# Sparse attention's blocks in another order, the memory branch's output weights kept on chip, and the attention branch's output projection cut into four parts, three of them between the attention blocks

## The chip, the cores and the metric

The kernel runs on one core of one Trainium2 chip. The metric is the device time of one execution in microseconds (us); lower is better.

## The reference, cut to what matters

One layer of an encoder step for 1024 prompt tokens and 64 sample tokens, all in float32. A projection feeds three branches and three gates:

```python
qa, ka, va, qi, ki, wi, ub, qm, gates = project_inputs(x, ...)
a = dsa_attend(qa, qi, wi, pos, ka, va, ki, topk)   # sparse attention: 8 heads of 64, 2 kv heads,
                                                    # keys = top 256 by an index score, chunk-causal
b = pool_mix(ub, ...)                               # trailing means over 2/4/8/16 frames
m = memory_attend(qm, mk, mv)                       # 4 heads of 128 over 256 memory tokens
ga, gb, gm = split(sigmoid(gates))
mixed = ga * (a @ w_oa) + gb * (b @ w_ob) + gm * (m @ w_om)
x = x + mixed @ w_out
h = rmsnorm(x, g_ffn)
y = x + (silu(h @ w_gate) * (h @ w_up)) @ w_down
```

`w_oa` and `w_om` are 512 x 1024, `w_out` 1024 x 1024; the keys, values and index keys are returned as well.

## The kernel before

Every float32 product runs as three products of a rounded high part and a remainder (hi x hi, hi x lo, lo x hi): `matmul3`, L120. A weight block comes by DMA into `raw` (3 buffers), `round_hi` makes `whi` (on POOL in the stage at hand, L96; on POOL or ACT later), and `lo_of` (L86, on DVE) makes `wlo`; `wblock` does all three, with two buffers each for `whi` and `wlo`. All DMAs are issued by SP in the order in which they stand on it. A scheduler places the instructions; each engine then runs its own list in order.

Activations are stored transposed, 128 channels by 1088 tokens, so a matmul streams tokens: 512, 384, 320, 288 or 256 columns. The stages that matter, in order:

1. Projections, index scores, top-k selection, pooling, memory attention, with gate matmuls as filling on TensorE. The memory branch's output sits in `bh`/`bl` (hi and lo).
2. **Memory merge units** (`fill_om(f, ci)`, L571): for one of 8 channel blocks `f` and one of 3 token chunks `OCH` (384, 384, 320 tokens) it loads gate and partial sum (`gt`, 4 buffers) from `side_m`, does 12 matmuls `bh`/`bl` x `w_om` into the bank `fl`, then DVE multiplies (L580), POOL adds (L581), and a DMA stores to `side_a`. There are 24, and the weights of a pair of blocks are loaded again for every chunk (12 loads). One unit runs ahead of the attention, three at its start, one behind each softmax.
3. **Sparse attention**, token blocks of 128 in the order 2, 0, 1, 3, 8, 4, 5, 6, 7 (block 8 is the 64 sample tokens; block b has 128(b+1) keys, block 8 has 192). For each block the queries are split and transposed (`queries_t`: ACT copy, DVE subtraction L879, 8 PE transposes L882, ACT copy). Then for each of the two kv heads a unit of two parts. `softmax`: PE logits L903 for 4 heads, on DVE one instruction that adds the selection and takes the extremum (L907, out `pr`), ACT exp L909, POOL reciprocal L911 and normalisation L913. `values`, which runs one unit behind: for each 128 keys 4 PE transposes (L926) into a bank, ACT copy `ph` L929, DVE remainder `pl` L86, two matmuls into `acc` L933; at its end ACT copies L935/L936, DVE adds L937/L938, ACT copy into `bh` L941 and DVE remainder into `bl`. The attention result overwrites the memory branch's in `bh`/`bl`, so a chunk's memory units must be done before. PSUM has 8 banks: 4 for `tr`, 2 for `mm`, one each for `fl` and `acc`. Once the memory units have run out, every third transposed block of `values` goes to `fl`.
4. **Attention merge** (L996 to L1010), after all blocks: for each `f` one load of gate and sum for all 1088 tokens (`side`, 3 buffers), and for 4 token chunks `ACH` (256, 256, 288, 288) 12 matmuls with `w_oa`, two DVE operations (L1005, L1006), ACT copy L1009 and DVE remainder into `mixed`, split into two token sets: 512 tokens (0) and 576 (1). As soon as the attention's memory is free, SP also issues the residual input (`y`, 16 loads, L990).
5. `out_proj(0)` and `out_proj(1)`: `mixed @ w_out` for a token set; the first needs all 8 channel blocks of `mixed` set 0. Then the norm and the feed-forward part to the end.

## Time and profile before

| | |
|---|---|
| three runs, us | 1764.99, 1768.73, 1771.66; median 1768.73 |
| profiled execution, us | 1774.77; its span 1772.7 |
| granted TensorE clock, mean of the span | 0.993 |
| busy: PE, PE weight load, DVE, ACT, POOL, us | 1719.6, 1668.6, 1124.5, 813.6, 409.5 |

The span is the stretch of one execution that the profiler covers, from the first to the last instruction; some 2 us lie around it. "Busy" of PE counts an instruction from its start to a modelled end, and matmuls overlap in the array, so it is more than the time that the array needs. "Idle before" a group is time in which its engine had nothing running, with what ended it.

### The profile page before, as it was taken

Reading aid. Unit: us, or ns where it says so; the run is one execution under the profiler, and the core shown is the slowest. Engines: PE = TensorE matmul, PEld = TensorE weight load, DVE = VectorE, ACT = ScalarE, POOL = GpSimd, SP = SyncE. Lnnn points to the kernel's source line nnn. Section 1 sums busy time; section 2 is a strip of 40 time slices with the busy share of each in tenths; the row PEclk is TensorE's granted clock in tenths of the full one; section 3 lists DMA queues with packets and bytes.
Section 4 is the critical chain, followed back from the end, with each engine's and each line's share of the span. In section 5 each row is a group of like instructions: output and inputs, shape, how many; then the busy total and the mean of one; then the engine's idle time right before and its main releaser. Section 6 shows DMA issues by size and latency. Waiting matters only on the chain.

```text
span 1772.7 us, 31533 instructions
## 1 busy us (share of the span) xinstructions
PE 1719.6 (97%) x11810; PEld 1668.6 (94%) x11810; DVE 1124.5 (63%) x2411; ACT 813.6 (46%) x1927; POOL 409.5 (23%) x444
## 2 busy tenths in 40 slices
PE   6999999999999998989899999999999999999999
PEld 6999999999999998877798999999999999999999
DVE  6567999999954433778783887544444454544443
ACT  5456677737523432569631354433333333433332
POOL 4111414355412213765203432110000000000000
PEclk9999999999999998999999999999999999999999
DMA  7222441232475336650354333222222221867673
GB/s 231 61 67 73 161 130 46 78 90 98 118 200 190 104 99 207 194 158 1 130 209 137 111 115 130 85 74 74 74 76 89 79 74 43 312 185 244 184 229 98
DMA packets 128582, 224.26 MB, mean 127 GB/s; under 512 B 23463, under 2 KB 86303, under 8 KB 128430
## 3 DMA queue, kind: packets, MB, share of 16 engines
q1 hardware_dynamic: 128430, 222.26, 39.0%
q8 instruction: 93, 1.52, 0.4%
q14 instruction: 59, 0.48, 0.1%
HBM read 167.84 MB, written 54.37 MB: 125 GB/s over the span
## 4 chain that ended last, share of the span: by engine, by line
PE 76%; DVE 11%; ACT 3%; issue 3%; DMA 3%; POOL 2%; SPq 0%; DVEq 0%; ACTq 0%; POOLq 0%
PE mm L1127 24%; PE mm L120 17%; PE mm L1275 15%; PE fl L120 13%; DVE junk_v L780 2%; ACT junk_a L777 2%; PE acc L933 1%; PE tr L903 1%; PE mm L333 1%; DVE wlo L86 1%; PE mm L926 1%; DMA gt<-side_m 1%; DVE lo L86 1%; DVE pl L86 1%; DVE tmlo L86 1%
## 5 line engine op out<-in xcount | busy, mean ns | idle before, releaser
L1127 PE MATMUL mm<-hi,whi 128*128 128x288 f32 (+1 forms) x1120 | 323.2, 289 | 1.1 <-DVE tu L1141 1.1
L1127 PE MATMUL mm<-hi,wlo 128*128 128x288 f32 (+1 forms) x1120 | 324.2, 290 | 0.0
L1127 PE MATMUL mm<-lo,whi 128*128 128x288 f32 (+1 forms) x1120 | 323.5, 289 | 0.0
L1127 PEld LDWEIGHTS mm<-hi,whi 128*128 128x128 f32 x1120 | 211.8, 189 | 1.8 <-DVE tu L1141 1.6
L1127 PEld LDWEIGHTS mm<-lo,whi 128*128 128x128 f32 x1120 | 211.8, 189 | 0.0
L1127 PEld LDWEIGHTS mm<-hi,wlo 128*128 128x128 f32 x1120 | 211.2, 189 | 0.4 <-DVE wlo L86 0.4
L120 PE MATMUL fl<-hh,whi 128*128 128x362 f32 (+1 forms) x576 | 189.7, 330 | 0.9 <-ACT hh L133 0.9
L120 PE MATMUL fl<-hl,whi 128*128 128x362 f32 (+1 forms) x576 | 189.8, 330 | 0.0
L120 PE MATMUL fl<-hh,wlo 128*128 128x362 f32 (+1 forms) x576 | 189.6, 330 | 0.0
L1275 PE MATMUL mm<-uh,wh 128*128 128x362 f32 (+1 forms) x512 | 167.4, 328 | 0.0
L1275 PE MATMUL mm<-ul,wh 128*128 128x362 f32 (+1 forms) x512 | 166.8, 326 | 0.0
L1275 PE MATMUL mm<-uh,wl 128*128 128x362 f32 (+1 forms) x512 | 166.0, 326 | 0.0
L86 DVE TENSOR_TENSOR wl<-raw,wh 128x1024 fp32r<-128x1024 f32 x64 | 78.4, 1225 | 123.4 <-ACT wh L94 123.3
L94 ACT CAST wh<-raw 128x1024 fp32r<-128x1024 f32 x64 | 67.3, 1051 | 145.6 <-PE mm L1275 137.5
L120 PE MATMUL mm<-tmlo,hh 128*128 128x256 f32 (+3 forms) x432 | 122.9, 286 | 1.5 <-DVE tmlo L86 1.5
L120 PE MATMUL mm<-tmhi,hh 128*128 128x256 f32 (+3 forms) x432 | 122.1, 288 | 2.0 <-POOL tmhi L96 2.0
L120 PE MATMUL mm<-tmhi,hl 128*128 128x256 f32 (+3 forms) x432 | 122.6, 286 | 0.0
L86 DVE TENSOR_TENSOR wlo<-raw,whi 128x1024 fp32r<-128x1024 f32 (+1 forms) x75 | 75.9, 1022 | 63.4 <-ACT whi L1119 37.5
L777 ACT ACTIVATE junk_a<-score,cand_a,sgn_a 128x512 f16<-128x512 f32 (+2 forms) x93 | 95.5, 1027 | 42.1 <-DVE cand_a L794 21.8
L120 PEld LDWEIGHTS fl<-hh,whi 128*128 128x128 f32 x576 | 108.3, 188 | 1.7 <-POOL rs L125 1.1
L120 PEld LDWEIGHTS fl<-hl,whi 128*128 128x128 f32 x576 | 108.2, 188 | 0.6
L120 PEld LDWEIGHTS fl<-hh,wlo 128*128 128x128 f32 x576 | 108.2, 188 | 0.5
(386 smaller groups left out, 4545.1 us busy)
## 6 DMA issues: line engine op xcount, KB each, us to landing
raw<-in_w_down_dram SPq DMA_DIRECT2D x66, 512.0 KB, 3.8
fraw<-in_w_gates_dram SPq DMA_DIRECT2D x24, 512.0 KB, 3.7
raw<-in_w_up_dram SPq DMA_DIRECT2D x22, 512.0 KB, 3.8
fr<-in_w_gate_dram SPq DMA_DIRECT2D x18, 512.0 KB, 3.7
side<-side_a SPq DMA_DIRECT2D x8, 1088.0 KB, 6.3
raw<-in_w_out_dram SPq DMA_DIRECT2D x16, 512.0 KB, 3.7
uf<-u SPq DMA_DIRECT2D x44, 181.0 KB, 3.7
u<-tg SPq DMA_DIRECT2D x22, 288.0 KB, 2.1
```

The lines of the kernel that those rows point to most:

```text
L86: V.tensor_tensor(lo, src, hi.bitcast(F32), op=OP.subtract)
L94: A.copy(hi, src)
L120: PE.matmul(ps, l, r, start=i == 0, stop=i == n - 1)
L333: PE.matmul(ps[:n, :cn], qt[:, h, :n], kstack[:, k0 + c:k0 + c + cn], start=True, stop=True)
L777: A.activation(junk[:n, :nk], sc, AF.Sign, bias=bj, scale=1.0 if scale is None else scale[:n, j:j + 1], accum_out=sj)
L780: V.tensor_scalar(junk[:n, :nk], sc, bj, None, op0=OP.is_ge, op1=OP.add, accum_out=sj)
L903: PE.matmul(lg[:n, i * 512:i * 512 + cn], qT[:, h, :n], kT[:, kv, s, k0 + c:k0 + c + cn], start=s == 0, stop=s == 1)
L926: PE.transpose(pt[:cn, i * n:(i + 1) * n], probs[i][:, c:c + cn], ident[:n, :n])
L933: PE.matmul(acc, vv, r, start=ji == 0 and i == 0, stop=ji == nj - 1 and i == 1)
L1127: PE.matmul(dst[i], l, r, start=start and j == 0, stop=stop and j == 11, skip_group_check=True)
L1275: PE.matmul(acc[f], l, r, start=kb == 0 and j == 0, stop=kb == NF - 1 and j == 2)
```

## The change

- The blocks run in the order 8, 6, 7, 2, 0, 1, 5, 4, 3; all keys are loaded ahead of the first or right behind its queries.
- The 24 memory merge units go by chunks 2, 0, 1, one more runs at the start, and two (three for block 2) behind each softmax. The weights `w_om` of a pair of blocks are loaded once and stay for the three chunks: 4 loads instead of 12, half of them in new tiles.
- 24 of the 32 attention merge units (chunks 3, 0 and 2 of `ACH`) move between the attention units, as the table `AFTER` says: `merge_unit` loads gate and sum into `ms` (4 buffers, in the memory weights' tiles), does its 12 matmuls into `fl`, DVE multiplies, POOL adds, and the sum is stored to `mix_d`. Each chunk loads its `w_oa` again: 16 loads instead of 4. While units are left, `values` uses `mm` alone.
- After the attention only chunk 1 (tokens 256 to 511) is merged; the sums of tokens 0 to 255 come back from `mix_d` in the same loop, those of 512 to 1087 inside `out_proj(0)` (`second_mixed`).
- Two remainders (`qs`, `bl`) and the add of the last merge move from DVE to POOL; `pr` has 10 buffers instead of 11; the queries come into `raw`.

```diff
     def fill_om(f, ci, other=False):
-        if f % 2 == 0:
-            om_w[ci] = wblock(a["w_om"][f:f + 2].rearrange("f p k j -> p f k j"), (2, 4, 128))
-        ow = om_w[ci]
+        if f not in om_w:
+            raw = raw_tile()
+            hi, lo = split_tiles() if f < 4 else [kv_p[0].tile([128, 1024], F32R, name=f"om{nm}{f}", tag=f"om{nm}{f}", bufs=1) for nm in "hl"]
...
+            om_w[f] = om_w[f + 1] = [t.rearrange("p (f k j) -> p f k j", f=2, k=4) for t in (hi, lo)]
+        ow = om_w[f]
...
-    rest = [(f, ci) for ci in range(3) for f in range(KT)]
+    OM_ORDER = (2, 0, 1)
+    rest = [(f, ci) for ci in OM_ORDER for f in range(KT)]
...
-    load_keys(0, 384)
+    load_keys(SEQ, SEQ + PAST + DEC)
+    load_keys(0, 512)
...
+    mix_d = dram.tile([KT, 128, T], F32, name="mix_d")
+    mrg = [(f, cc) for cc in (3, 0, 2) for f in range(KT)]
...
-    KEYS_AT = {0: (384, 768), 3: (768, SEQ + PAST + DEC)}
+    KEYS_AT = {8: (512, SEQ)}
...
-            return ap_.tile([128, 1024], F32, name=name, tag="pr", bufs=11)
+            return ap_.tile([128, 1024], F32, name=name, tag="pr", bufs=10)
...
-            q = ap_.tile([128, HA, HDA], F32, name="q", tag="q", bufs=2)
+            q = raw_tile()[:, :512].rearrange("p (h d) -> p h d", h=HA)
...
-            V.tensor_tensor(qs[:n, :, 1], q[:n], qs[:n, :, 0].bitcast(F32), op=OP.subtract)
+            G.tensor_tensor(qs[:n, :, 1], q[:n], qs[:n, :, 0].bitcast(F32), op=OP.subtract)
...
-                    pt = mm() if rest or ji % 3 != 2 else fps(512)
+                    pt = mm() if rest or mrg or ji % 3 != 2 else fps(512)
...
-                lo_of(aol[:, cs, t0:t0 + n], av, aoh[:, cs, t0:t0 + n])
+                G.tensor_tensor(aol[:, cs, t0:t0 + n], av, aoh[:, cs, t0:t0 + n].bitcast(F32), op=OP.subtract)
...
+        MS_TAGS = [f"om{nm}{f}" for f in (4, 6) for nm in "hl"]
+
+        def merge_unit(f, cc):
+            if (f, cc) not in oa_w:
+                oa_w[f, cc] = oa_w[f + 1, cc] = wblock(a["w_oa"][f:f + 2].rearrange("f p k j -> p f k j"), (2, 4, 128))
+            ow = oa_w[f, cc]
+            c0, cn = ACH[cc]
+            tag = MS_TAGS[len(mrg) % 4]
+            t = kvp.tile([128, 1024], F32, name="ms", tag=tag, bufs=1)[:, :2 * cn].rearrange("p (s t) -> p s t", s=2)
+            SP.dma_start(t, side_a[f, :, :, c0:c0 + cn].rearrange("s p t -> p s t"))
+            ps = fps(cn)
+            matmul3(ps, [(ow[0][:, f % 2, k], ow[1][:, f % 2, k], aoh[:, k, c0:c0 + cn], aol[:, k, c0:c0 + cn]) for k in range(4)])
+            V.scalar_tensor_tensor(t[:, 0], t[:, 0], 1.0, ps, op0=OP.add, op1=OP.mult)
+            G.tensor_tensor(t[:, 1], t[:, 1], t[:, 0], op=OP.add)
+            SP.dma_start(mix_d[f, :, c0:c0 + cn], t[:, 1])
...
-        for b in (2,0,1,3,8,4,5,6,7):
+        AFTER = {(0, 0): 2, (0, 1): 2, (1, 0): 2, (1, 1): 2, (5, 0): 1, (5, 1): 1, (4, 0): 2, (4, 1): 2, (3, 0): 4, (3, 1): 6}
+        for b in (8, 6, 7, 2, 0, 1, 5, 4, 3):
             qT = queries_t(b)
...
-                fill(-1, 1)
+                fill(-1, {2: 3}.get(b, 2))
+                merges(AFTER.get(todo[:2], 0))
...
+    c0, c1 = ACH[1][0], ACH[2][0]
     for f in range(KT):
-        sides = row.tile([128, 2, T], F32, name="side", tag="side", bufs=3)
-        SP.dma_start(sides, side_a[f].rearrange("s p t -> p s t"))
+        sides = row.tile([128, 3, 256], F32, name="side", tag="side", bufs=4)
+        SP.dma_start(sides[:, :2], side_a[f, :, :, c0:c1].rearrange("s p t -> p s t"))
+        SP.dma_start(sides[:, 2], mix_d[f, :, :c0])
...
+        keep_mixed(f, 0, c0, sides[:, 2])
+        G.tensor_tensor(pin, pin, gt, op=OP.add)
+        keep_mixed(f, c0, c1, pin)
...
+    def second_mixed(f):
+        pin = y0p.tile([128, 576], F32, name="pin", tag="pin", bufs=3)
+        SP.dma_start(pin, mix_d[f, :, c1:])
+        keep_mixed(f, c1, T, pin)
...
-    sq0 = out_proj(0)
+    sq0 = out_proj(0, {f: lambda f=f: second_mixed(f) for f in range(KT)})
```

What moves, at three places. **POOL**, around the softmaxes of blocks 0 and 1 (lines 911 and 913 before are 921 and 923 now). Before:

```order
L911 TENSOR_TENSOR sm<-sm,mone 128x4
L96 TENSOR_SCALAR whi<-raw 128x1024
L913 TENSOR_SCALAR pr<-pr,sm 128x128 x4
L581 TENSOR_TENSOR gt<-gt 128x384 x2
L911 TENSOR_TENSOR sm<-sm,mone 128x4
L913 TENSOR_SCALAR pr<-pr,sm 128x128 x4
```

The same place now (`ms` is a merge unit's gate and sum, `bl` the attention result's remainder, `qs` the queries'):

```order
L923 TENSOR_SCALAR pr<-pr,sm 128x128 x4
L978 TENSOR_TENSOR ms<-ms 128x288
L889 TENSOR_TENSOR qs<-raw,qs 128x8x64
L952 TENSOR_TENSOR bl<-ot,bh 128x2x128
L96 TENSOR_SCALAR whi<-raw 128x1024
L978 TENSOR_TENSOR ms<-ms 128x288 x2
L921 TENSOR_TENSOR sm<-sm,mone 128x4
L96 TENSOR_SCALAR whi<-raw 128x1024
L952 TENSOR_TENSOR bl<-ot,bh 128x2x128
L923 TENSOR_SCALAR pr<-pr,sm 128x128 x4
```

Between one normalisation and the next stand now up to eight other instructions, and `whi` and `bl` between a reciprocal and its normalisation. **PE**, the last unit of the attention and what follows it. Before, the last `values` blocks of block 7 and the start of the merge:

```order
L926 MATMUL mm<-ident,pr 128x128 x4
L933 MATMUL acc<-ph,vb 128x512
L933 MATMUL acc<-pl,vb 128x512
L933 MATMUL acc<-ph,vb 128x512
L933 MATMUL acc<-pl,vb 128x512
L933 MATMUL acc<-ph,vb 128x512
L933 MATMUL acc<-pl,vb 128x512
L120 MATMUL mm<-bh,whi 128x256
L120 MATMUL mm<-bl,whi 128x256
L120 MATMUL mm<-bh,wlo 128x256
```

Now, where 72 merge matmuls of 288 columns in a row end with the first two of these rows:

```order
L120 MATMUL fl<-bl,whi 128x288
L120 MATMUL fl<-bh,wlo 128x288
L936 MATMUL fl<-ident,pr 128x128 x4
L943 MATMUL acc<-ph,vb 128x512
L943 MATMUL acc<-pl,vb 128x512
L943 MATMUL acc<-ph,vb 128x512
L943 MATMUL acc<-pl,vb 128x512
L120 MATMUL mm<-bh,whi 128x256
L120 MATMUL mm<-bl,whi 128x256
L120 MATMUL mm<-bh,wlo 128x256
```

Six merge units now stand ahead of the last two key blocks' values, all through the one bank `fl`; behind them 96 merge matmuls of 256 columns are left where 384 stood. **SP**, from the end of the attention on. Before:

```order
L997 DMA side<-side_a 128x2x1088 x3
L990 DMA y_10646<-in_x_t_dram 128x576 x6
L990 DMA y_10656<-in_x_t_dram 128x512 x7
L990 DMA y_10646<-in_x_t_dram 128x576
L990 DMA y_10656<-in_x_t_dram 128x512
L990 DMA y_10646<-in_x_t_dram 128x576
L997 DMA side<-side_a 128x2x1088
L110 DMA raw<-in_w_out_dram 128x1024
```

Now (`pin` is what `second_mixed` fetches):

```order
L110 DMA raw<-in_w_out_dram 128x1024
L1024 DMA y_11103<-in_x_t_dram 128x576 x6
L1024 DMA y_11113<-in_x_t_dram 128x512 x7
L1024 DMA y_11103<-in_x_t_dram 128x576
L1024 DMA y_11113<-in_x_t_dram 128x512
L1024 DMA y_11103<-in_x_t_dram 128x576
L1054 DMA pin<-mix_d 128x576 x3
L110 DMA raw<-in_w_out_dram 128x1024
L1038 DMA side<-side_a 128x2x256
L1039 DMA side<-mix_d 128x256
```

The sides of the first three (now four) channel blocks stand ahead of the 16 loads of `y`, the others behind them, now also behind three loads of `pin`.

## Rows read from the trace of the kernel before

**Rows 1.** The page: busy us (share of the span) and instructions of each engine.

```profile
PE 1719.6 (97%) x11810; PEld 1668.6 (94%) x11810; DVE 1124.5 (63%) x2411; ACT 813.6 (46%) x1927; POOL 409.5 (23%) x444
```

**Rows 2.** Busy us (instructions) by stretch, granted clock, DMA share, GB/s.

```profile
core 0: us, PE busy (x) PEld busy (x) DVE busy (x) ACT busy (x) POOL busy (x), PEclk, DMA share, GB/s
690.00:723.00 33.00, 27.65 (x137) 24.64 (x135) 20.83 (x50) 14.04 (x41) 18.05 (x19) 0.79 0.80 275
723.00:789.00 66.00, 59.51 (x369) 52.71 (x370) 51.79 (x124) 38.49 (x104) 49.34 (x59) 0.97 0.65 201
789.00:877.00 88.00, 81.83 (x480) 65.21 (x478) 77.93 (x153) 74.56 (x154) 40.40 (x45) 1.00 0.11 40
877.00:883.00 6.00, 4.02 (x18) 3.73 (x19) 2.09 (x7) 1.14 (x3) 0.00 (x0) 0.72 0.67 188
930.00:980.00 50.00, 50.00 (x237) 41.64 (x236) 18.56 (x22) 9.91 (x14) 17.24 (x12) 1.00 0.43 140
```

**Rows 3.** The chain that ended last: start us, us, what.

```profile
691.44 6.98 DMA gt<-side_m
763.73 3.49 DMA side_a<-gt
767.23 3.62 DMA gt<-side_m
879.48 101.06 PE mm L120 x624
```

**Rows 4.** Timeline of PE, one `values` part: start us, us, what.

```profile
845.35 0.40 PE L933 MATMUL acc<-pl,vb 128*128 128x512 f32 x1
845.59 0.60 PE L926 MATMUL fl<-ident,pr 128*128 128x128 f32 x4
845.94 0.48 PE L933 MATMUL acc<-ph,vb 128*128 128x512 f32 x1
```

**Rows 5.** Groups of DVE, 690 to 880.

```profile
L86 DVE TENSOR_TENSOR pl<-mm,ph 128x512 fp32r<-128x512 f32 x58 | 39.0, 686 | 6.4 <-ACT ph L929 5.8
L86 DVE TENSOR_TENSOR wlo<-raw,whi 128x1024 fp32r<-128x1024 f32 x12 | 17.3, 1442 | 0.4 <-POOL whi L96 0.3
L86 DVE TENSOR_TENSOR bl<-ot,bh 128x256 fp32r<-128x256 f32 x16 | 8.9, 555 | 2.9 <-ACT bh L941 2.9
L879 DVE TENSOR_TENSOR qs<-q,qs 128x512 fp32r<-128x512 f32 x8 | 6.0, 751 | 2.0 <-ACT qs L878 1.1 <-PE fl L120 0.7
```

**Rows 6.** Groups of POOL, 690 to 890; the last two of 985 to 1070.

```profile
L911 POOL TENSOR_TENSOR sm<-sm,mone 128x4 f32<-128x4 f32 x16 | 17.6, 1100 | 42.1 <-ACT pr L909 30.0 <-DVE bl L86 4.6 <-DVE pl L86 4.0
L96 POOL TENSOR_SCALAR whi<-raw 128x1024 fp32r<-128x1024 f32 x10 | 10.7, 1066 | 7.3 <-DMA gt<-side_m 2.6 <-PE fl L120 2.4 <-issue 2.1
...
L1090 POOL TENSOR_TENSOR ws<-fr 128x288 f32<-128x288 f32 x4 | 9.6, 2395 | 19.9 <-DVE fr L1083 19.9
...
L1090 POOL TENSOR_TENSOR ws<-fr 128x256 f32<-128x256 f32 x4 | 3.5, 872 | 4.3 <-DVE fr L1083 4.3
```

**Rows 7.** Ends of attention units on DVE: start us, us.

```profile
724.43 0.43 DVE L938 TENSOR_TENSOR ot<-acc,ot 64x256 f32<-64x256 f32 x1
...
878.91 0.43 DVE L938 TENSOR_TENSOR ot<-acc,ot 64x256 f32<-64x256 f32 x1
```

**Rows 8.** SP around the merge, and how long a load of y took.

```profile
877.70 10.04 SPq L990 DMA_DIRECT2D y<-in_x_t_dram  x16
889.73 0.38 SPq L997 DMA_DIRECT2D side<-side_a  x1
...
DMA to landing us min/median/max: 2.9/6.7/8.2
```

**Rows 9.** DVE's groups of the merge, 880 to 932.

```profile
L1005 DVE SCALAR_TENSOR_TENSOR side<-side,mm 128x256 f32<-128x256 f32 x16 | 6.7, 418 | 5.0 <-PE mm L120 2.7 <-DMA y<-in_x_t_dram 2.2
L86 DVE TENSOR_TENSOR xl<-side,xh 128x256 fp32r<-128x256 f32 x16 | 6.6, 418 | 0.0
```

**Rows 10.** Durations by tile: ns min/median/max, first and last start.

```profile
L86 DVE TENSOR_TENSOR bl<-ot,bh x18: 280/422/1240, 725.5 to 879.8; 128x256 fp32r<-128x256 f32 x16, 128x128 fp32r<-128x128 f32 x2
L581 POOL TENSOR_TENSOR gt<-gt x22: 867/1014/2071, 694.2 to 780.0; 128x384 f32<-128x384 f32 x14, 128x320 f32<-128x320 f32 x8
```

More of the change, by code (lines that the diff above doesn't have):

```diff
@@ L941, in values, with merges @@
                 A.copy(aoh[:, cs, t0:t0 + n], av)
-                lo_of(aol[:, cs, t0:t0 + n], av, aoh[:, cs, t0:t0 + n])
+                G.tensor_tensor(aol[:, cs, t0:t0 + n], av, aoh[:, cs, t0:t0 + n].bitcast(F32), op=OP.subtract)
         todo = None
-        for i in range(3):
+        for i in range(4):
             fill_om(*rest.pop(0), other=i % 3 > 0)
         def fill(upto, n=0):
-            while rest and (n > 0 or rest[0][1] <= upto):
+            while rest and (n > 0 or OM_ORDER.index(rest[0][1]) <= upto):
                 fill_om(*rest.pop(0))
                 n -= 1
-        for b in (2,0,1,3,8,4,5,6,7):
+        oa_w = {}
+        MS_TAGS = [f"om{nm}{f}" for f in (4, 6) for nm in "hl"]
[12 more added lines that the diff above has]
+            SP.dma_start(mix_d[f, :, c0:c0 + cn], t[:, 1])
+        def merges(n):
+            for _ in range(n):
+                merge_unit(*mrg.pop(0))
+        AFTER = {(0, 0): 2, (0, 1): 2, (1, 0): 2, (1, 1): 2, (5, 0): 1, (5, 1): 1, (4, 0): 2, (4, 1): 2, (3, 0): 4, (3, 1): 6}
+        for b in (8, 6, 7, 2, 0, 1, 5, 4, 3):
             qT = queries_t(b)
```

28 lines of the change are left out of this document (15 added, 13 removed).

## The prediction

> **What bounds the kernel now.** I read the page's busy shares first: PE is busy 97% of the span, DVE 63%, ACT 46%, POOL 23% [rows 1]. An average over stages does not say where PE is short of work, so the stretches come next. Where `out_proj` runs, from 930 to 980, PE is busy 50.00 of 50 at full clock [rows 2]; there only fewer matmuls can help, and both kernels' lists hold the same number of matmul columns. In the attention PE shows 27.65 of 33.0, 59.51 of 66 and 81.83 of 88, with its weight load at 65.21 in the last [rows 2]. These are too kind: a matmul of 512 columns is drawn 0.40 long, while the next thing starts 0.24 behind it, and four transposes take 0.35 from start to start [rows 4]. The columns have a better price in the chain, 101.06 us for 624 matmuls in which PE never lets go [rows 3]; these are 216,576 columns by the order list, so 0.467 ns each. At that price, with 0.084 a transpose, the attention from 690 to 877 holds some 144 us of PE work in 187 us. Some 43 us of holes are what the change can fill.
>
> Why the holes are there is seen in the order lists priced by row means. I cut each engine's list at the 18 attention units' ends and summed each piece: PE 137.6 us in all, DVE 158.9, ACT 135.4, POOL 93.3. Taking the largest engine of each piece gives 170.6. After the first unit, which ends at 724.9, measured time is 154.4 (to 879.3 [rows 7]) against 147.6 of the pieces: 127.5 against 129.2 up to 854, then 20.2 against 25.2 in the last three units, where nothing is left but the chain of transpose, copy, remainder, product. So the attention goes by DVE and ACT in its late part and by PE in the units with memory merges, and pieces tell it to 2% except at its two ends. At the start the chain waits 6.98 us for a `gt` load [rows 3], DMA busy 0.80 and the clock at 0.79 [rows 2], the full level in part only: the first unit's PE work, 16.1 us, begun at 694.9, should end at 711.0 and ends at 724.9, 13.9 late.
>
> **The change, part by part.** *Merge units into the attention.* Of 384 merge matmuls (104,448 columns, 48.8 us) 288 move, 79,872 columns or 37.3 us; 96 of 256 columns (11.5 us) stay. The same cut on the new lists gives PE 176.2, DVE 160.3, ACT 134.8, POOL 159.8, and 198.4 for the largest of each piece. Of these 23.1 are the first piece, where POOL's share starts ahead of the stage, so I take PE's 16.7 there; 175.3 follow. One piece as an example, unit (5,1): 36 merge matmuls or so 4.2, logits 2.1, 24 transposes 2.0, twelve products 2.8, query transposes 0.7, together PE 11.8, DVE 9.8, POOL 9.8, ACT 7.5. Before, unit (7,0) had PE 6.4 and DVE 6.8: eight `pl` of 0.686 [rows 5], two adds of 0.43 [rows 7], `bl`.
>
> *Prices on DVE and POOL.* DVE loses nine `qs` at 0.751, 18 `bl` at 0.555 and eight `wlo`, and gains 24 multiplies at about 0.45 (a 256-column one is 0.418 [rows 9]) and twelve `wlo` at 1.442 [rows 5]: about even. POOL gains nine `qs`, 18 `bl`, 24 adds and four `whi` at 1.066 [rows 6]. No row has these adds on POOL in the attention. The nearest below is 0.872 for 256 columns alone, the nearest above 2.395 for 288 columns, beside DVE's `fr` [rows 6]; in between lies the memory unit's add in this very stage, median 1.014 for 384 and 320 columns, once 2.071 [rows 10]. I take 0.86, 0.95 and for `qs`, twice the size, 1.67, as they are nearest to that median: 56 us more on POOL. Now POOL's reciprocal waits 42.1 us, 30.0 of them for ACT [rows 6], and POOL is busy 18.05 of 33, 49.34 of 66, 40.40 of 88 [rows 2]; the room is there on the whole. But in units (2,0) to (1,1) POOL is the largest in half of the pieces, 42.4 against PE's 32.4 and DVE's 36.0, and behind each `ms` add stands a normalisation for which the next `values` wait.
>
> Two remainders moved off DVE touch a row that I can show: `bl` on DVE ranges from 0.280 to 1.240 [rows 10], so something holds it up. The Trainium skill, "SBUF — State Buffer", section "Who interferes with whom", says that a DVE instruction with two SBUF inputs contends with a GpSimd instruction that reads SBUF; the spread of `bl` beside `pl`, whose one input is in PSUM and which lies close to its mean, agrees. By that rule each of sixteen `wlo` could wait for one POOL instruction, some 16 us on DVE at most by the rows' prices, and POOL's adds could wait as well.
>
> *The start.* Memory units of 320 tokens come first (−1.6 us at half level), the queries and keys are issued sooner, weights of later units are not reloaded. Of the 13.9 I leave 9: the loads themselves remain. If none went the first unit would end 4.9 later, if all went 9 earlier. First unit: 694.9 − 1.6 + 16.7 + 9 = 719.0.
>
> *The DMAs added.* 24 loads of gate and sum (6.9 MB), stores of sums (3.3 MB), and four weight loads more. From 789 to 877 the share was 0.11, 40 GB/s [rows 2]: hidden. But a memory unit's recycle, store 3.49 and reload 3.62 [rows 3], shows what the four `ms` tiles can cost when units stand close: seven us for four units, while four take 6.4 on PE. That matters in the last unit, (3,1): six in a row through the one bank `fl`, each 1.6 of PE and 0.45 of DVE before the bank is free. With the 5.0 of the old tail I put 6 on the end.
>
> Attention: 719.0 + 175.3 + 6 = 900.3, against 879.3: **+21.0**.
>
> *What is left of the merge.* Before, 48.8 us of columns and 1.7 of clock (0.72 over 6 us [rows 2]) lay between the last unit and `out_proj(0)`: 50.5. Now PE has 11.5 us, then waits for the sides. The 16 loads of `y`, issued over 10.04 us from 877.70, land in up to 8.2 [rows 8]; they are 4.46 MB. Sides 4 to 7 (1.57 MB) stand behind these, three `pin` (0.88) and one `w_out` (0.52): 7.4 MB. At the 344 GB/s of a full share (275 at 0.80) that is 21.6 us, at 281 (188 at 0.67 [rows 2]) 26.4. I take 22.5 behind the last product for side 7, then multiply 0.42, POOL's add 0.87, copy, remainder 0.418 [rows 9], with their waits 2.6: at +25.1. By then PE has done 21 of the first 24 `out_proj` matmuls, 5.0 us; with 1.7 for the clock the stage is effectively at +21.8. **−28.7**. Were everything there in time it would be 50.5 − 13.2, −37.3; with the slower rate −24. Before, the sides behind `y` were late too, but three channel blocks of 6 us covered them: DVE waited 2.2 us for `y` [rows 9].
>
> *The second set inside `out_proj(0)`.* Eight copies and eight remainders of 576 columns, less than 1 us each; there DVE is busy 18.56 of 50 and ACT 9.91 [rows 2], so PE's products hide them. Without cover they would cost some 7 us.
>
> Sum: +21.0 − 28.7 = −7.7 on the profiled span of 1772.7. The profiled run took 1774.77 and the median is 1768.73, so I put the difference on the median: **1761**.
>
> **The rivals.** *PE takes all of it.* If DVE, ACT and POOL fit into each other's pieces, since softmax and values overlap one unit apart, the stage goes by PE alone: 694.9 − 1.6 + 176.2 + 9 + 5 = 883.5, only 4.2 later, −24.5 in all, 1744. For it: PE's work now exceeds DVE's by 16. Against: the old attention, with DVE at 158.9, took 154.4 from the first unit's end, longer than any one engine's sum of that stretch, so engines did not fit.
>
> *No change.* The extra pieces lose a little each: `values` has two banks where every third block also had `fl`, `pr` ten tiles instead of eleven, `gt` and `ms` are recycled. Some 0.45 us in each of 18 units eats the 7.7: 1769.
>
> *Slower: POOL's line.* POOL works in order, and up to eight instructions now stand between two normalisations. If 24 `ms` adds and 18 `bl` go at 2.395 instead of 0.95 and 0.86, POOL gets 63 us more; laid on the pieces where it is the largest or nearly, 34 of them come through (19 in the first six units, 4 in the middle, 11 later): 1795. It is slower than before by over 0.5% (about what a measurement of this kernel can tell from no change) once 17 us come through, at a mean add of about 1.7. Against it speaks the memory unit's median of 1.014 with as much DVE work beside it.
>
> **How the numbers follow.** The forecast, 1753 to 1768, has 0.40; its band is the start's and the loads' bounds, +5, −9 and −9, +5, which rarely fall together. PE alone, 1744, 0.22. No change, 1766 to 1777, 0.21. POOL, 1778 to 1795, 0.17. The range 1742 to 1778 leaves the last and little below. Faster than 1759.9 is the second case and 0.24 of the forecast: 0.46; same 0.37; slower 0.17.
>
> **What would show it.** In the changed profile: the last product of the attention near 900 (883 for PE alone, from 917 for POOL); POOL's groups `ms`, `bl` and `qs` at 0.95, 0.86 and 1.67, and PE's idle time before transposes put down to normalisations if they are dearer; the first unit's end near 719; PE idle for some 8 to 13 us between the merge's 96 matmuls and the end of `out_proj`'s first 24, released by a side's load; the start of `out_proj` effectively 22 behind the last product; PE full from there on, and the rest of the span as long as before. I am wrong if the holes turn out to be waits that a fuller PE lengthens, or if the sides come late by another road.

## The result

The changed kernel took 1785.1 us (median of 4 runs, 1781.8 to 1786.76) where the kernel before took 1768.93: ratio 1.0091, 95% interval 1.0065 to 1.0116. It is slower by some 16 us; the forecast was 1761. Its profiled execution took 1783.65 us, span 1781.8, so the two traces differ by 9 us only: before's profiled run lay 6 us above its median. What follows explains the 9 us that the traces show, and uses medians and ratios for verdicts.

The page's line on the engines answers to [rows 1]:

```profile
PE 1723.2 (97%) x11810; PEld 1670.3 (94%) x11810; DVE 1111.7 (62%) x2348; ACT 812.3 (46%) x1919; POOL 458.5 (26%) x507
```

The windows of the attention and of what follows (as in [rows 2]; the attention now ends at 918.8):

```profile
core 0: us, PE busy (x) PEld busy (x) DVE busy (x) ACT busy (x) POOL busy (x), PEclk, DMA share, GB/s
690.00:720.00 30.00, 25.87 (x153) 23.77 (x152) 14.62 (x44) 10.60 (x35) 17.06 (x23) 0.89 0.72 222
720.00:758.00 38.00, 38.00 (x220) 34.49 (x220) 25.95 (x48) 22.03 (x44) 24.34 (x25) 1.00 0.57 170
758.00:800.00 42.00, 40.25 (x244) 33.55 (x242) 28.57 (x62) 27.19 (x60) 24.82 (x26) 1.00 0.43 128
800.00:845.00 45.00, 40.10 (x264) 35.02 (x265) 34.73 (x84) 33.83 (x88) 41.12 (x54) 1.00 0.48 147
845.00:889.00 44.00, 40.37 (x269) 34.34 (x268) 35.47 (x71) 29.29 (x65) 30.09 (x36) 1.00 0.46 135
889.00:919.00 30.00, 21.69 (x127) 18.25 (x126) 16.44 (x24) 6.07 (x13) 12.40 (x16) 0.91 0.48 152
919.00:925.00 6.00, 6.00 (x32) 6.00 (x33) 1.43 (x4) 1.55 (x5) 0.73 (x1) 0.60 0.97 336
925.00:945.00 20.00, 17.93 (x107) 15.23 (x106) 17.85 (x28) 9.39 (x19) 10.37 (x10) 1.00 1.06 387
```

Three things are to be seen. From 720 to 758, where block 6 stands beside memory units, PE is busy without a break. From 889 to 919 no engine is: PE 21.69 of 30, DVE 16.44. And behind the attention DMA's share is 0.97 and 1.06, at 336 and 387 GB/s, where it was 0.65 over the 49 us of the old merge:

```profile
880.00:929.00 49.00, 49.00 (x381) 49.00 (x380) 38.53 (x96) 14.27 (x32) 1.06 (x1) 0.97 0.65 231
```

The granted clock falls twice there: 0.91 from 889 to 919, where PE had the gaps shown below, and 0.60 from 919 to 925. At the lower level those two stretches lose at most 2.7 and 2.4 us (their length times the missing share).

The unit ends on DVE (as [rows 7]; the first unit of the new order has 64 tokens) give the split that the rest of this text uses:

```profile
719.93 0.29 DVE L948 TENSOR_TENSOR ot<-acc,ot 64x128 f32<-64x128 f32 x1
...
918.36 0.43 DVE L948 TENSOR_TENSOR ot<-acc,ot 64x256 f32<-64x256 f32 x1
```

Before: first unit 724.9, last 879.3, 154.5 between them, 893.4 from there to the end. Now: 720.2, 918.8, 198.6 and 863.0. The attention from its first unit's end grew by 44.1, the rest shrank by 30.4. The first unit's end moved by 4.7 in these two traces, but traces of kernels that are alike up to there put it between 720.0 and 724.4, so that part is not resolved.

POOL's groups in the attention (as [rows 6], 690 to 925) answer to the costs that were bounded:

```profile
L978 POOL TENSOR_TENSOR ms<-ms 128x288 f32<-128x288 f32 x16 | 12.8, 805 | 12.2 <-DVE ms L977 10.7 <-issue 1.6
L952 POOL TENSOR_TENSOR bl<-ot,bh 128x256 fp32r<-128x256 f32 x16 | 11.8, 736 | 6.9 <-ACT bh L951 6.9
L889 POOL TENSOR_TENSOR qs<-raw,qs 128x512 fp32r<-128x512 f32 x8 | 10.4, 1301 | 1.8 <-ACT qs L888 1.8
...
L978 POOL TENSOR_TENSOR ms<-ms 128x256 f32<-128x256 f32 x8 | 7.7, 963 | 6.0 <-DVE ms L977 6.0
```

PE's timeline at the tail, the six units in a row (only the rows that begin a stretch; brackets hold the idle time before and who ended it):

```profile
900.55 0.40 PE L120 MATMUL fl<-bh,whi 128*128 128x288 f32 x1 [1.38 <-DVE ms L977]
...
903.04 0.37 PE L120 MATMUL fl<-bh,whi 128*128 128x288 f32 x1 [0.64 <-DVE ms L977]
...
905.69 0.40 PE L120 MATMUL fl<-bh,whi 128*128 128x288 f32 x1 [0.83 <-DVE ms L977]
...
908.19 0.37 PE L120 MATMUL fl<-bh,whi 128*128 128x288 f32 x1 [0.64 <-DVE ms L977]
...
910.55 0.40 PE L120 MATMUL fl<-bh,whi 128*128 128x288 f32 x1 [0.55 <-DVE ms L977]
...
913.08 0.66 PE L936 MATMUL fl<-ident,pr 128*128 128x128 f32 x4 [0.67 <-DVE ms L977]
914.47 0.50 PE L943 MATMUL acc<-ph,vb 128*128 128x512 f32 x1 [0.73 <-ACT ph L939]
915.97 0.50 PE L943 MATMUL acc<-pl,vb 128*128 128x512 f32 x1 [1.00 <-DVE pl L86]
...
918.94 0.55 PE L120 MATMUL mm<-bh,whi 128*128 128x256 f32 x1 [1.87 <-DVE ot L948]
```

Each unit waits for the multiply that frees the one bank: 2.5 us from unit to unit for 1.6 of matmuls, 4.7 of gaps in all. Ahead of the longest gap, 1.38, that multiply itself stood behind a remainder of weights on DVE (898.31 in the last section's rows). Then the last values, which stood behind the units, take 5.9 with little to overlap.

### The profile page after: what moved, and what is told of

The parts are those of the page before. It is cut to its first block, busy times and chain, and to the rows that moved or that the text cites. A ratio compares the mean times of both kernels' runs of the same rounds, so it can differ in the third digit from the quotient of the medians.

```text
span 1781.8 us, 31724 instructions
## 1 busy us (share of the span) xinstructions
PE 1723.2 (97%) x11810; PEld 1670.3 (94%) x11810; DVE 1111.7 (62%) x2348; ACT 812.3 (46%) x1919; POOL 458.5 (26%) x507
## 4 chain that ended last, share of the span: by engine, by line
PE 60%; DVE 4%; POOL 3%; DMA 3%; issue 3%; ACT 1%; SPq 0%; DVEq 0%; POOLq 0%; ACTq 0%
PE mm L1170 24%; PE mm L1318 14%; PE fl L120 10%; PE mm L120 7%; PE acc L943 1%; PE tr L913 1%; PE mm L936 1%; POOL pr L923 1%; DVE lo L86 1%; DVE wlo L86 1%; DMA y<-in_x_t_dram 1%; POOL sm L921 1%; DMA pin<-mix_d 0%; PE mm L620 0%; DVE fr L1126 0%
## 5 line engine op out<-in xcount | busy, mean ns | idle before, releaser
L1318 PE MATMUL mm<-ul,wh 128*128 128x362 f32 (+1 forms) x512 | 166.8, 326 | 0.0
L86 DVE TENSOR_TENSOR wlo<-raw,whi 128x1024 fp32r<-128x1024 f32 (+1 forms) x77 | 81.4, 1068 | 66.7 <-ACT whi L1162 37.5
```

The costliest lines, as they stand in the source:

```text
L86: V.tensor_tensor(lo, src, hi.bitcast(F32), op=OP.subtract)
L1318: PE.matmul(acc[f], l, r, start=kb == 0 and j == 0, stop=kb == NF - 1 and j == 2)
```

## The experiments

18 kernels ran. "Attention" is from the first unit's end to the last's, "rest" from there to the end of the span, both in the one trace of each kernel; the ratio is to the kernel before on the same chip. Where two kernels run the same instructions, a unit's length repeats to about 0.1 us from trace to trace; the first unit's end does not. A unit is named by block and kv head: (6,0) is block 6's first.

| kernel | attention | rest | median us | ratio, 95% interval |
|---|---|---|---|---|
| before | 154.5 | 893.4 | 1768.93 | 1 |
| changed | 198.6 | 863.0 | 1785.1 | 1.0091 (1.0065 to 1.0116) |
| order_only | 160.2 | 891.4 | 1774.82 | 1.0035 (1.0022 to 1.0049) |
| move8 | 166.8 | 879.2 | 1769.84 | 1.0006 (0.9992 to 1.0019) |
| move16 | 180.1 | 868.5 | 1771.46 | 1.0013 (1.0000 to 1.0026) |
| pool_undone | 195.7 | 867.0 | 1784.45 | 1.0071 (1.0045 to 1.0098) |
| tail_banks | 194.1 | 865.3 | 1783.76 | 1.0091 (1.0067 to 1.0115) |
| y_behind | 198.9 | 862.3 | 1784.46 | 1.0094 (1.0072 to 1.0117) |
| m16_no_wlo | 173.9 | 868.0 | 1765.43 | 0.9979 (0.9962 to 0.9995) |
| m16_no_mm | 176.0 | 868.2 | 1768.04 | 1.0001 (0.9985 to 1.0018) |
| m16_no_prep | 174.7 | 870.0 | 1766.7 | 0.9993 (0.9980 to 1.0005) |
| m16_no_add | 177.4 | 868.3 | 1770.19 | 1.0016 (1.0004 to 1.0028) |
| old_order | 146.7 | 891.2 | 1764.72 | 0.9979 (0.9967 to 0.9991) |
| order_rate1 | 161.7 | 891.8 | 1775.85 | 1.0042 (1.0028 to 1.0056) |
| old_rate2 | 146.7 | 891.2 | 1763.75 | 0.9978 (0.9967 to 0.9990) |
| old_order_dve | 151.7 | 891.3 | 1767.57 | 1.0011 (0.9997 to 1.0026) |
| old_two_banks | 160.0 | 893.8 | 1778.91 | 1.0070 (1.0049 to 1.0090) |
| old_move8 | 171.6 | 880.7 | 1778.79 | 1.0073 (1.0054 to 1.0092) |
| old_move8_three | 163.0 | 881.7 | 1768.54 | 1.0014 (1.0001 to 1.0027) |
| after_three | 200.2 | 867.0 | 1788.52 | 1.0125 (1.0107 to 1.0143) |

### How many units are moved

The first three keep everything but the moved units, of which 0, 8 or 16 are left; the others go back behind the attention, into a loop like the old one.

```diff
# order_only
-    mrg = [(f, cc) for cc in (3, 0, 2) for f in range(KT)]
+    mrg = []
-        AFTER = {(0, 0): 2, (0, 1): 2, (1, 0): 2, (1, 1): 2, (5, 0): 1, (5, 1): 1, (4, 0): 2, (4, 1): 2, (3, 0): 4, (3, 1): 6}
+        AFTER = {}
# move8
+    mrg = [(f, 3) for f in range(KT)]
+        AFTER = {(0, 0): 2, (0, 1): 2, (1, 0): 2, (1, 1): 2}
# move16
+    mrg = [(f, cc) for cc in (3, 0) for f in range(KT)]
+        AFTER = {(0, 0): 2, (0, 1): 2, (1, 0): 2, (1, 1): 2, (5, 0): 1, (5, 1): 1, (4, 0): 2, (4, 1): 2, (3, 0): 2}
```

order_only: 

> The new block order, the kept memory weights, the larger memory part at the start and the two remainders on POOL stay; none of the 24 merge units moves, all 32 stand behind the attention as before. Theory A (moved units lengthen the attention one for one, and what was lost beyond that is the last unit and the wait for the sides): the attention ends near 877, that is 918.8 less 37.3 of columns and about 5 of the gaps between the six units in a row, and the time is 1762 to 1768, a few us under before by the shorter start. Theory B (POOL's longer line holds the softmax up): the remainders are still on POOL, so the attention ends at 885 or later and the time is 1772 or more. Theory C (the new order itself is worse, whatever is moved): 1775 or more.

move8: 

> Only the 8 merge units of the last token chunk (800 to 1087) stand between the blocks, two behind each unit of blocks 0 and 1; 24 stand behind the attention. Theory A: the attention ends 11 to 14 us later than with none moved (8 units of 12 matmuls of 288 columns are 12.9 us) and the time is within 4 us of that kernel. If holes take the moved work: 5 us later or less, and 8 us or more faster than with none moved. Theory B: more than 15 us later, since 8 adds on POOL come on top.

move16: 

> The merge units of tokens 800 to 1087 and 0 to 255 stand between the blocks, none behind the last unit; tokens 512 to 799 are merged behind the attention with 256 to 511. Theory A: against the changed kernel the six units in a row are gone (6 to 9 us) and the sides have 24 more us of matmuls to hide behind instead of 11.5 (4 to 6 us): 1770 to 1776. If the loss is spread over all moved units, 16 of 24 keep two thirds of it: 1779 or more.

Measured, step by step: the first eight units lengthen the attention by 6.6 us (12.9 of columns) and shorten the rest by 12.2; the second eight by 13.3 (11.5 of columns) against 10.7; the last eight, in the tail, by 18.5 (12.9) against 5.5. By medians −5.0, +1.6 and +13.6. So only the first eight pay, and even they lengthen the attention by half of their columns; the last eight make the change what it is. Up to block 4 the changed kernel's units are as long as move16's, and block 3 takes 30.1 us for 11.9. order_only itself is slower than before, which theory A had not foreseen: 154.5 became 160.2 with as many matmuls.

### POOL's line

```diff
-            G.tensor_tensor(qs[:n, :, 1], q[:n], qs[:n, :, 0].bitcast(F32), op=OP.subtract)
+            V.tensor_tensor(qs[:n, :, 1], q[:n], qs[:n, :, 0].bitcast(F32), op=OP.subtract)
-                G.tensor_tensor(aol[:, cs, t0:t0 + n], av, aoh[:, cs, t0:t0 + n].bitcast(F32), op=OP.subtract)
+                lo_of(aol[:, cs, t0:t0 + n], av, aoh[:, cs, t0:t0 + n])
-        G.tensor_tensor(pin, pin, gt, op=OP.add)
+        V.tensor_tensor(pin, pin, gt, op=OP.add)
```

pool_undone: 

> The changed kernel with the two remainders (queries and attention result) and the add of the last merge back on DVE; the adds of the moved units stay on POOL. Theory B: POOL loses some 25 us of work in the attention and its line is shorter ahead of each normalisation: 1775 or less. Theory A: POOL is not what the late units wait for, DVE gains 16 us of work: between 1783 and 1792.

1784.45 against 1785.1, and 2.9 us less of attention: theory B's 10 us are not there, and the rows above say why: POOL's adds took 0.81 and 0.96, not 2.4. But this run exchanges POOL's work for DVE's and does not price POOL's line alone. The chain that ended last runs for 48 us of the attention over POOL in the changed kernel, 6 before and 9 here, while DVE's part of it rises from 12 to 35. POOL's adds of the moved units were also left out alone, on move16:

```diff
-            G.tensor_tensor(t[:, 1], t[:, 1], t[:, 0], op=OP.add)
-            SP.dma_start(mix_d[f, :, c0:c0 + cn], t[:, 1])
+            SP.dma_start(mix_d[f, :, c0:c0 + cn], t[:, 0])
```

m16_no_add: 

> The kernel with 16 units moved, whose moved units leave out POOL's add of the gate and sum (16 instructions of 0.8 to 1.0 us). Theory B2 (POOL's line counts in the blocks with moved units, although the remainders back on DVE gained nothing): attention shorter by 5 us or more. Theory D (DVE and the chain count): by less than 3 us.

2.7 us less of attention, and a median 1.3 lower; the ratio, 1.0016 against 1.0013, did not fall. The adds are a small part at most.

### The tail and the sides

tail_banks gives every second unit of the tail a bank of `mm`; y_behind puts the loop that loads `y` behind the loop over the sides and gives the sides seven buffers.

```diff
# tail_banks
-            ps = fps(cn)
+            ps = mm()[:, :cn] if len(mrg) in (0, 2, 4) else fps(cn)
# y_behind
-    for k in range(KT):
-        for i, (t0, n) in enumerate(SETS):
-            SP.dma_start(ys[i][:, k], a["x_t"][k][:, t0:t0 + n])
...
-        sides = row.tile([128, 3, 256], F32, name="side", tag="side", bufs=4)
+        sides = row.tile([128, 3, 256], F32, name="side", tag="side", bufs=7)
...
+    for k in range(KT):
+        for i, (t0, n) in enumerate(SETS):
+            SP.dma_start(ys[i][:, k], a["x_t"][k][:, t0:t0 + n])
```

tail_banks: 

> The changed kernel, with three of the six merge units in a row behind the last softmax (every second one) in a bank of mm instead of all six through fl. Theory A1 (the single bank costs the gaps in the tail): the gaps between the six units, 4.7 us in the profile, mostly go, the attention ends at 913 to 915 and the time falls by 4 to 5 us, to about 1780. Rival (the units wait for their weights and their ms tiles): the gaps stay, under 1.5 us gained.

y_behind: 

> The changed kernel, with the 16 loads of the residual input behind the 16 loads of the sides (7 side buffers instead of 4). Theory A2 (the sides come late because they stand behind those loads): PE's 8.0 us lost in the 30 us behind the attention fall to 2 or 3, and the time falls by 4 to 6 us, to about 1780. Rival (the transfers are bound by their bytes, and the three loads of pin and the residual input are late in turn, so that out_proj waits for them): under 2 us gained.

With the second bank the attention got 4.5 shorter, as A1 said, but the rest 2.3 longer, and the ratio stayed at 1.0091. y_behind gained nothing either. The windows behind the attention in these two (tail_banks, then y_behind) are as full of transfers as the changed kernel's:

```profile
916.00:941.00 25.00, 20.54 (x116) 17.08 (x116) 17.78 (x30) 10.24 (x22) 10.66 (x11) 0.84 0.97 343
```

```profile
928.00:948.00 20.00, 17.67 (x106) 15.21 (x105) 18.71 (x27) 8.81 (x17) 11.56 (x10) 1.00 0.96 345
```

Some 10 MB (sides, `y`, `pin`, weights) come in while PE has 11.5 us of merge left. In the changed kernel the chain that ended last goes over these loads for 25.0 of the 29.4 us from 918.9 on:

```profile
918.90 6.24 DMA y<-in_x_t_dram
925.16 4.06 DMA y<-in_x_t_dram
932.02 6.09 DMA side<-side_a
938.17 5.86 DMA pin<-mix_d
945.54 2.73 DMA pin<-mix_d
```

y_behind does not show that bytes are all there is to it. There SP issued seven of the eight sides from 887 to 894, ahead of `y` (920 to 930), and the chain from 922 to 952 holds no transfer: it goes over PE's merge, DVE's remainders, POOL's adds of the sides and ACT, and the rest of the span is only 0.7 shorter. So where the sides come early, the merge's own small operations take about the same time; the rival's forecast of the time holds, its reason is not shown.

### What a moved unit costs

On move16, three parts of the moved units are left out in turn: the remainders of their weights (the high part is used twice), ten of their twelve matmuls, and their whole preparation (weights of the memory units are used). Like m16_no_add they serve as prices alone. `half_block` is `wblock` without the remainder; it returns the high part twice.

```diff
# m16_no_wlo
-                oa_w[f, cc] = oa_w[f + 1, cc] = wblock(a["w_oa"][f:f + 2].rearrange("f p k j -> p f k j"), (2, 4, 128))
+                oa_w[f, cc] = oa_w[f + 1, cc] = half_block(f)
# m16_no_prep
+                oa_w[f, cc] = oa_w[f + 1, cc] = om_w[f % 4]
# m16_no_mm
-            matmul3(ps, [(ow[0][:, f % 2, k], ow[1][:, f % 2, k], aoh[:, k, c0:c0 + cn], aol[:, k, c0:c0 + cn]) for k in range(4)])
+            PE.matmul(ps, ow[0][:, f % 2, 0], aoh[:, 0, c0:c0 + cn], start=True, stop=False)
+            PE.matmul(ps, ow[1][:, f % 2, 3], aol[:, 3, c0:c0 + cn], start=False, stop=True)
```

m16_no_wlo: 

> The kernel with 16 units moved, but the remainders of the moved units' weights are left out (8 DVE subtractions of 1.5 us; the high part stands in their place in the products), so that DVE has some 12 us less and PE as much as before. Theory D (in the late blocks DVE is what a moved unit lengthens, by its remainder of the weights and its multiply, and this is why the second 8 units cost their full length): the attention shrinks by 6 us or more. Theory A (PE's own time in its fixed order): by less than 2 us.

m16_no_mm: 

> The kernel with 16 units moved, but of each moved unit's 12 matmuls only 2 are left (its weights, loads, multiply, add and store stay), so that PE has 20 us less to do in the attention. Theory A: PE's time comes out nearly one for one in blocks 5, 4 and 3 and by about half in blocks 0 and 1, the attention shrinks by 13 us or more. Theory D: DVE and the softmax chain hold the blocks at their length, it shrinks by 6 us or less.

m16_no_prep: 

> The kernel with 16 units moved, whose moved units take the weights that lie ready from the memory units, so that 8 loads, 8 roundings on POOL and 8 remainders on DVE are left out (the products are of the wrong weights). Theory D (the preparation is what a moved unit costs): attention shorter by 10 us or more, as without the remainders (6.2) and some 4 for the roundings, 1760 to 1763. If only DVE's remainders count: 6 to 7, 1764 to 1767, as without these alone.

160 matmuls less, 43,520 columns or 20.3 us at the price of [rows 3], shortened the attention by 4.1 us. Eight remainders less, some 12 us on DVE, shortened it by 6.2, and leaving out the loads and POOL's roundings too by no more (5.4). Theory A falls, and D holds with this limit: the preparation counts through DVE's remainders alone. The last three blocks (5, 4 and 3) in move16 and in m16_no_mm, where 79 matmuls less leave the stretch almost as long:

```profile
844.30:900.10 55.80, 48.42 (x298) 39.75 (x298) 42.21 (x82) 35.10 (x79) 32.52 (x40) 0.97 0.38 120
```

```profile
845.50:898.80 53.30, 41.37 (x219) 30.37 (x219) 40.33 (x82) 34.73 (x78) 32.36 (x40) 0.97 0.40 124
```

If they add up (each is from one trace, and the adds' 2.7 is not borne out by the ratio), matmuls, remainders and adds make 13.0 of the 19.9 us by which move16's attention is longer than order_only's. The other 7 were not taken apart; they hold the multiplies and the bank that `values` lacks while merge units are left (below).

### The order

old_order is order_only with the old order of blocks, of memory chunks and of key loads, and one memory unit behind each softmax.

```diff
# old_order, from order_only
-        for b in (8, 6, 7, 2, 0, 1, 5, 4, 3):
+        for b in (2, 0, 1, 3, 8, 4, 5, 6, 7):
...
-    OM_ORDER = (2, 0, 1)
+    OM_ORDER = (0, 1, 2)
...
-                fill(-1, {2: 3}.get(b, 2))
+                fill(-1, 1)
```

old_order: 

> The kernel with no merge unit moved, in the order of before (2, 0, 1, 3, 8, 4, 5, 6, 7), memory chunks 0, 1, 2 and one memory unit behind each softmax; the kept memory weights, the remainders on POOL and the four units at the start stay. Theory E (the light blocks 2, 0, 1 have room for filling and the heavy blocks 6 and 7 have none, so the new order makes the 24 memory units cost their full length): against the kernel with the new order and no merge unit moved it is 5 to 10 us faster, 1764 to 1770, and against the kernel before the same or up to 5 us faster, as eight preparations of weights are gone. Theory C2 (what the order-only kernel loses is the remainders on POOL and the ten pr tiles): 1772 to 1777, as with the new order.

146.7 against 160.2, and 1764.72 against 1774.82: the order of the blocks, with the orders of chunks and keys that go with it, costs 10 to 13 us. Of the kernels that leave nothing out, this one and old_rate2 below are the fastest tried, 0.2% under the one before. Two stretches of each show where it comes from, old_order first: units (2,1) to (1,1), then (6,0) to (7,1).

```profile
722.40:758.90 36.50, 36.02 (x231) 33.54 (x230) 22.84 (x66) 22.74 (x61) 27.52 (x38) 1.00 0.57 164
831.70:869.10 37.40, 31.89 (x182) 25.02 (x181) 29.64 (x51) 27.72 (x55) 16.66 (x17) 1.00 0.25 95
```

The same units in order_only, and then its heavy stretch cut into block 6 and block 7:

```profile
806.20:841.30 35.10, 27.64 (x154) 20.47 (x154) 27.47 (x67) 31.58 (x75) 27.90 (x35) 1.00 0.23 76
731.20:801.60 70.40, 67.94 (x404) 58.80 (x402) 45.32 (x93) 43.50 (x91) 39.60 (x42) 1.00 0.30 94
...
731.20:776.50 45.30, 45.30 (x275) 41.84 (x274) 27.85 (x50) 26.12 (x49) 26.59 (x28) 1.00 0.40 127
776.50:801.50 25.00, 22.64 (x131) 16.96 (x129) 17.38 (x44) 17.28 (x42) 12.91 (x15) 1.00 0.11 34
```

What touches the bank `fl` tells the memory units' matmuls from the rest (the columns are PE, its weight loads, DVE, ACT): old_order's light blocks, then order_only's blocks 6 and 7.

```profile
722.40:758.90 36.50, 23.37 (x132) 21.02 (x132) 5.73 (x11) 0.00 (x0) 1.00 0.57 164
...
731.20:776.50 45.30, 23.97 (x122) 20.58 (x120) 5.51 (x10) 0.00 (x0) 1.00 0.40 127
776.50:801.50 25.00, 0.06 (x1) 0.00 (x0) 0.55 (x1) 0.00 (x0) 1.00 0.11 34
```

In old_order the light blocks hold 132 of these matmuls, in order_only block 6 holds 120 (two more touch the window's edge); in both cases that is 46,080 columns, 21.5 us at the price of [rows 3]. The light blocks take 36.5 us with them and 35.1 without, with 55 more matmuls of the attention's own in their place. Block 6 takes 45.3 us with them, PE busy throughout, and 20.7 in old_order without: there they cost their full length. (Neighbouring units overlap, so a stretch also holds work of the next one; only the sum of 13.5 is free of that.) Blocks 3, 4 and 5 give 17.7 us back, 40.6 for 58.3.

Block 7 is another matter. It holds no memory matmul in order_only, and takes 25.0 us where it takes 16.8 in old_order. All its 16 transposed blocks go to the two banks of `mm`: whether `values` may use `fl` is settled by where the program stands, and there memory units are still left, while the scheduler has run them all by the end of block 6. old_two_banks (below), without a memory unit in these blocks, takes 22.8 us for block 7, so the lack of the bank is some 6 of the 8.2. A kernel that gives it back in block 7 alone was not tried.

The rate of memory units was a rival, tried in both orders by `fill(-1, 1)` in order_only and `fill(-1, {2: 3}.get(b, 2))` in old_order:

order_rate1: 

> The kernel with the new order and no merge unit moved, but with one memory unit behind each softmax (besides those that a block's values force), instead of two and three. Theory F (the order is harmless; two units behind each softmax use all 24 up in blocks 8 and 6, where PE is then full, and leave the gaps of blocks 7, 2, 0, 1, 5, 4 and 3 empty): the attention, 160.2 us from the first unit's end with two, falls to 152 or less, the time to 1764 to 1769. Theory E (only the light blocks take filling): most of the memory units still stand in heavy blocks or in lumps, attention 156 or more, time 1771 to 1775.

old_rate2: 

> The kernel with the old order and no merge unit moved, but with two memory units behind each softmax (three in block 2) instead of one. Theory F: the units are used up sooner, their last ones in the first light blocks, and the later gaps stay empty: attention 4 us or more above 146.7, time 1769 or more. Theory E: they all still stand in the light blocks, attention 146 to 149, time 1764 to 1767.

Theory F falls: 161.7 and 146.7, as without the edit. The heavy units are as long to 0.1 us, as the scheduler places the memory units alike at either rate; so the rate was hardly tried.

old_order_dve takes the edit of pool_undone on old_order.

old_order_dve: 

> The kernel with the old order and no merge unit moved, with the two remainders and the last merge's add back on DVE; of the change it keeps the memory weights held for three chunks, the four units at the start, the ten pr tiles and the queries in raw. If the kept weights make that kernel faster than before: the same time, 1763 to 1767. If the remainders on POOL do, since DVE is the largest in the late blocks: attention 4 us or more longer, 1768 or more.

5.0 us more of attention, 2.9 of median, and a ratio of 1.0011 for 0.9979. The remainders on POOL, which the forecast feared, are what makes old_order faster than before.

### The third bank

old_move8 is old_order with the eight units of tokens 0 to 255 moved; the program has one behind each softmax of blocks 4 to 7.

old_move8: 

> The kernel with the old order and kept weights, with 8 merge units (tokens 0 to 255, 11.5 us of columns) moved among blocks 4 to 7, one behind each softmax; 24 units stand behind the attention. Theory E (the late heavy blocks have gaps on PE that a moved unit does not fill, since each brings DVE work too): the attention grows by 9 us or more over 146.7, the rest falls by 10 to 12, the time is 1762 to 1768, no gain of more than 3 us over that kernel. Rival (with the memory units in the light blocks the late gaps are free for merge units): the attention grows by 5 us or less and the time is 1757 to 1761.

24.9 us longer for 11.5 of columns, more than any theory said. The trace shows that the units did not run where the program has them. These are the instructions on `fl` in blocks 1, 3 and 8, then in blocks 4 to 7:

```profile
738.10:805.20 67.10, 31.03 (x194) 27.33 (x192) 7.72 (x17) 0.00 (x0) 0.95 0.54 164
805.20:892.80 87.60, 1.69 (x8) 1.06 (x8) 1.37 (x2) 1.18 (x2) 1.00 0.16 56
```

The scheduler ran all eight ahead of block 4. Blocks 1, 3 and 8 are 12.7 us longer than in old_order, and blocks 4 to 7, without a moved unit in them, 12.1. So this run says nothing of moved units in the late blocks; it raised the question of the bank that `values` gives up while the program has merge units left:

```diff
# old_two_banks, from old_order
-                    pt = mm() if rest or mrg or ji % 3 != 2 else fps(512)
+                    pt = mm()
# old_move8_three, from old_move8, and after_three, from the changed kernel
+                    pt = mm() if rest or ji % 3 != 2 else fps(512)
```

old_two_banks: 

> The kernel with the old order, kept weights and nothing moved, with every transposed block of values in the two banks of mm, where every third goes to fl once the memory units have run out. Theory G (the third bank is worth about 1 us in each unit of the late blocks, so that whoever moves merge units among them pays for the bank): attention 8 to 12 us above 146.7, time 1772 to 1777. Rival (the banks count for nothing, a unit waits for DVE): under 3 us, 1763 to 1768.

old_move8_three: 

> The kernel with the old order and 8 merge units moved, with every third transposed block of values in fl throughout, beside the merge units. Theory G: the attention, 171.6 without it, falls by 6 us or more, the time to 1773 or less. Rival: by less than 3 us, since merge units and transposed blocks wait for one another in fl, 1776 to 1782.

after_three: 

> The changed kernel, with every third transposed block of values in fl as soon as the memory units have run out, beside the merge units. Theory G: the attention from the first unit's end, 198.6, falls by 5 us or more, the time to 1780 or less. Rival: by less than 2 us, 1782 to 1788.

In the old order G holds: 13.3 us for the bank without a unit moved. Some of it is clock, which was granted at 0.92 in blocks 6 and 7 of old_two_banks and at 1.00 in old_order: at most 3.9 of the 48.2 us that these two blocks took. Block 6 and block 7 there:

```profile
836.70:862.10 25.40, 21.74 (x107) 15.35 (x105) 18.82 (x33) 18.40 (x36) 11.07 (x12) 0.96 0.34 132
862.10:884.90 22.80, 18.72 (x84) 12.98 (x84) 11.97 (x21) 9.87 (x20) 5.38 (x6) 0.87 0.03 7
```

With the bank given to `values` beside the merge units, 8.6 of the 24.9 come back, but old_move8_three differs from old_move8 in more than the bank: seven of its eight units do run in blocks 4 to 7. These blocks take 88.8 us with them, 75.4 in old_order: 13.4 for 10.0 of columns, so the late blocks' gaps took nothing of these units, as theory E had said of old_move8.

The changed kernel gains nothing from it: units (2,1) to (1,1) become 7 us shorter and (3,1) 4.6, but (5,0) and (3,0) 14 longer, where units and transposed blocks now share the one bank. So the bank is a real price in this program, and handing it back is no cure where merge units hold it.

## Why the prediction was wrong

**The holes.** "Some 43 us of holes are what the change can fill" is the step that failed. The attention was forecast as 719.0 + 175.3 + 6, the largest engine of each piece. From the first unit's end it took 198.6 where 181.3 stood: against the pieces, of the 17.3, 6.1 lie in block 3, which took 30.1 where 18.0 and the 6 for the tail were allowed, and 13.3 in blocks 8, 6, 7, 5 and 4; blocks 2, 0 and 1 were 2 shorter. PE's lost time from 690 to the attention's end, counted as the gaps between starts beyond the price of the columns, was 50.8 us before and 53.1 after: 37.3 us of work went in and nothing was filled on balance. A piece's largest engine is a bound that holds only if the other engines' work hides in it; m16_no_mm shows it does not, since taking 20.3 us from PE, the largest, gave 4.1. The median missed by 24.1 us, of which 16.8 are in the traces; the other 7.3 come from the base, as the forecast kept the median 5.8 below the profiled run, and the changed kernel's lies 1.5 above it.

**The order.** It was costed at its start alone (−5.9; traces of the new order have it from −0.5 to −4.9). It moved memory units from blocks where they are nearly free to block 6, where they cost their length, and left block 7 without its third bank: +13.5 between old_order and order_only. In the changed kernel block 6's units took 28.4 and 17.0 us, 10.1 and 8.6 before.

**The tail.** 6 us were allowed for the bank and the old tail; the gaps are 4.7 and the last values 5.9, as described, but they come on top of each other. The last eight units cost 18.5 and gave back 5.5.

**The merge.** −28.7 forecast, −30.4 measured: the size is right, the mechanism in part. The chain does go over the loads, 25.0 of 29.4 us. But PE's idle pieces between 919 and 951 add to 4.1 us, where 8 to 13 were named as the sign, and none was ended by a side's load:

```profile
928.16 0.39 PE L120 MATMUL mm<-bh,wlo 128*128 128x256 f32 x1 [0.60 <-DVE wlo L86]
932.24 0.39 PE L120 MATMUL mm<-bh,wlo 128*128 128x256 f32 x1 [0.94 <-DVE wlo L86]
938.76 0.50 PE L120 MATMUL mm<-xh,wlo 128*128 128x512 f32 x1 [0.53 <-DVE wlo L86]
947.39 0.50 PE L120 MATMUL mm<-xh,whi 128*128 128x512 f32 x1 [0.43 <-ACT whi L94]
950.31 0.50 PE L120 MATMUL mm<-xh,wlo 128*128 128x512 f32 x1 [1.60 <-DVE wlo L86]
```

More went with the clock, 0.60 from 919 to 925. And y_behind, with seven sides in early, is only 0.7 shorter there, so the sides' wait is not the only thing of that length.

**The prices.** POOL's adds were 0.81 and 0.96 for 0.95 and 0.86, `bl` 0.74 for 0.86, `qs` 1.30 for 1.67: all near or under the value taken. The contention that was bounded by 16 us cost little over the price taken: 14 `wlo` of 1.545 in the attention, for 1.442. The slower rival, POOL's line, ended on the right side for the wrong reason: its price of 2.395 an add was not there, and that 1785.1 lies in its range is luck. The rival "no change" named the banks at 0.45 us a unit; in the old order they are worth up to 13.3 in its late blocks, some three times that a unit. And DVE, called "about even", was where a moved unit hurt most, by its remainders of weights that are fetched again for every chunk.

Still open: how much of the 13.5 us of the order is the bank beyond some 6 us in block 7 (in block 6 PE is full as well), what POOL's line costs by itself, and how the 7 us of move16 split.

## What to carry to other kernels

Idle time of an engine is room only where the added work's other parts (a remainder, a multiply, a bank) find room too: price a moved unit on every engine and bank it touches, and ask which blocks are short of work rather than how much is idle in all. Filling work that already lies in the right place is lost when blocks change order. What is moved out of a stage takes with it the cover of that stage's loads and small operations: count what must still land and be worked off in what is left. And where a scheduler places the work, look in the trace where it ran: old_move8's units ran in other blocks than the program has them, and a bank that is given up in program order was missing long after the units were done.
